# Five more dense U products ahead of the scatter, in homes taken from the scatter's share of memory

## The chip, the cores and the metric

The kernel runs on one core of a Trainium2 chip. The metric is the device time of one execution in microseconds (us). TensorE is called PE here, VectorE DVE, ScalarE ACT, GpSimd POOL, and SyncE, which issues most of the DMAs, SP.

## The reference, cut to what matters

One layer of a hybrid encoder over 512 tokens of width 1024: a mixer (RG-LRU and convolution), then PEER, a retrieval over 128 x 128 single-neuron experts, then a norm. The change touches PEER alone:

```python
q = (x @ w_q)                                    # 8 heads, 2 halves of 128
s = q . sub_keys                                 # 128 scores for each half
s1, i1 = top_k(s[:, :, 0], 16); s2, i2 = top_k(s[:, :, 1], 16)
top_s, pos = top_k(all s1 + s2, 16)              # 16 experts for each head and token
gate = softmax(top_s);  idx = 128 * i1 + i2
act = gelu(u[idx] . x)
out = sum over the 16 and the heads of gate * act * v[idx]
```

## The kernel before, in words

For 384 of the 512 tokens PEER is computed densely: for each of 128 columns of experts (128 experts each) a **U product** `gelu(u . x)` of 128 experts by 384 tokens, times a dense matrix of gates, times the V rows. The other 128 tokens gather their experts' rows one by one, later, beside the dense V loop. The trunk is in float32 precision: each operand is split into a high and a low part, and a product is three matmuls for each of eight slices, so 24 matmuls of 384 columns.

The order of the work in the stretch around the change:

1. **Routing.** Sixteen half-heads hp. For each: `query` (24 matmuls of 512 columns), the scores, then `rank` on DVE (top 16 of each of four token blocks). Behind some of them `choose` merges two halves into experts and gates, on DVE, ACT and POOL. Its first step on ACT is the cast `ii` (line 511), which reads the ranks' result. `US[hp]` says how many U products are written behind the scores of hp, ahead of the `choose` that follows. With one at the start (`EARLY`) these are products u0 to u22. For a U product in the routing ACT casts the high part (`w_hi`, line 108), POOL subtracts the low part (`w_lo`, line 110), PE multiplies (lines 464 to 466), ACT applies gelu (line 473).
2. **Scatter.** 3 token blocks of 8 steps, 16 tokens each. `turned(b)` makes the operand `trb` of a block by three PE transposes (line 624); the second and third block's are made behind the fifth step of the block before. Each step builds one-hot matrices on DVE (`hot` line 647, twice; `oa` line 651, six times; two buffers each, one for eight tokens), multiplies them on PE (`p_g`, line 657, 48 matmuls), copies the result out on ACT (`stg`) and writes it to memory (`scr_g`, line 661). Behind each step stands one U product, until 46 are made: u23 to u45 behind steps 1 to 23. Here DVE makes `w_lo`, not POOL.
3. **Tail.** u46 to u50 behind the scatter, with `w_lo` on POOL again, while the gates `g_s` come back from `scr_g` (line 726). They can be loaded only when the last step is written.
4. **Dense V loop.** 128 turns: `weigh` multiplies a U product by its gates (line 730) and splits it (`wt_hi`, `wt_lo`); PE multiplies by V (`po`, line 758); a later U product follows in each turn.

U products live in SBUF until they are weighed. u0 to u7 use spare gather buffers, the rest one of 44 `homes`: the first `HOMES_NOW` in pool `wk` (`w_e`), which is there during the routing, the next in `wk2` (`w_f`), opened when the routing's memory is given back, the last three in `wk3` (`w_g`), behind the scatter. Three more buffer counts matter: `w_hi` and `w_lo` have three buffers, raw weights five, and the PSUM tile `p_e` two. `p_e` is shared by the U products and the transposes of `turned`.

Waits and the order on each engine's queue are made by the framework when the kernel is built: it takes what is written first as more urgent, and lets a later instruction go ahead where, by its own estimate of durations, the earlier one isn't ready. On the chip each engine then runs its queue strictly in that order.

Of the kernel before, what the change touches and what calls it, by code (L numbers as in the profile page):

```python
# [60 lines left out]
def tile_kernel(ctx, tc, x, par, wi, bd, kd, mg, wo, wq, keys, u_rows, v_rows, u_t, v_t, fg, ffg, sel, out):  # L61
# [384 lines left out]
    AHEAD_W = 2  # L446
    EARLY = 1

    US = (0, 0, 0, 1, 1, 2, 1, 2, 1, 2, 1, 2, 1, 2, 1, 5)
    us = {}  # L450

    HOMES = AHEAD_U + 1 - 8
    HOMES_NOW = 15

    LAG = AHEAD_U - HOMES - 3
    HOMES_END = 3
    homes = [(wk, "w_e", HOMES_NOW)]

    def dense_u(i, eng):
        hi, lo = split(load(u_t[i].rearrange("p c e -> p (c e)")), eng)  # L460
        p = ps_e.tile([P, TD], F32, name="p_e")
        for c in range(NC):
            cs = slice(c * P, (c + 1) * P)
            nc.tensor.matmul(p, hi[:, cs], m_hi[:, c, :TD], start=(c == 0), stop=False)  # L464
            nc.tensor.matmul(p, hi[:, cs], m_lo[:, c, :TD], start=False, stop=False)  # L465
            nc.tensor.matmul(p, lo[:, cs], m_hi[:, c, :TD], start=False, stop=(c == NC - 1))  # L466
        if i < len(spare):
            w = spare[i]
        else:
            k = (i - len(spare)) % HOMES  # L470
            pool, name, n = homes[(k >= HOMES_NOW) + (k >= HOMES - HOMES_END)]
            w = pool.tile([P, NT, GT], F32, name=name, bufs=n)
        nc.scalar.activation(flat(w), p, AF.Gelu_apprx_tanh)  # L473
        us[i] = w
# [21 lines left out]
    def rank(rp, v, i, src):  # L496
        s2 = rp.tile([P, NK], F32, name="s2")
        best16(v, i, src, s2)
# [58 lines left out]
    with ExitStack() as rt:  # L557
# [25 lines left out]
        for hp in range(16):  # L583
# [9 lines left out]
            for b in range(NB):  # L593
                rank(rp, v16[:, hp // 2, b, hp % 2], i16[:, hp // 2, b, hp % 2], s[:, b])
            for _ in range(US[hp]):
                dense_u(len(us), nc.gpsimd)
# [7 lines left out]
    wk2 = ctx.enter_context(tc.tile_pool(name="wk2", bufs=1))  # L604
    homes.append((wk2, "w_f", HOMES - HOMES_NOW - HOMES_END))
    TURN = 4
# [267 lines left out]
```

## Time and profile before

| | us |
|---|---|
| median of 3 runs | 1566.47 (1563.59 to 1568.61) |
| the profiled execution: time | 1564.53 |
| its span, first to last instruction | 1562.8 |

PE is busy 94% of the span, DVE 79%, ACT 41%, POOL 42%. Times inside the profile are us from the start of the span. Routing with U products runs from about 267 to 487, the scatter to about 669, the V loop from 689 to the end.

### The profile page before, as it was taken

How to read it: one execution, taken by the hardware profiler on the slowest of the kernel's cores; microseconds unless marked ns; L12 is line 12 of the kernel's file. 1: busy time of each engine (PE TensorE's matmuls, PEld its weight loads, DVE VectorE, ACT ScalarE, POOL GpSimd, SP SyncE). 2: the span in 40 equal slices, each digit the busy share in tenths (PEclk: the TensorE clock that was granted, in tenths of full speed). 3: DMA queues.
4: the chain of work that ended last, by engine and by line, in shares of the span. 5: the costliest groups of instructions: out<-in, count | busy, mean ns of one | idle time of the engine just before them, and what ended most of it. 6: DMA issues, size and time to landing. Idle time of an engine off the chain costs nothing.

```text
span 1562.8 us, 21636 instructions
## 1 busy us (share of the span) xinstructions
PE 1475.6 (94%) x7939; PEld 1294.8 (83%) x7939; DVE 1230.5 (79%) x2255; ACT 636.4 (41%) x937; POOL 653.0 (42%) x382
## 2 busy tenths in 40 slices
PE   5987889999988999999899999999999999999997
PEld 4764657899977889898799999999999999888886
DVE  6995745599999999948777787777777877777776
ACT  5458443344434554442233333333333333333333
POOL 3644722476551000144455555445444444444440
PEclk9998879999989999999899999999999999999999
DMA  6220412323223666589999899998989988777783
GB/s 235 87 75 14 174 42 96 114 101 103 88 96 113 224 209 230 209 254 368 334 325 344 295 340 302 334 325 301 347 300 345 320 308 308 284 276 275 263 290 134
DMA packets 137787, 358.69 MB, mean 230 GB/s; under 512 B 10064, under 2 KB 59472, under 8 KB 134352
## 3 DMA queue, kind: packets, MB, share of 16 engines
q1 hardware_dynamic: 100240, 222.03, 41.8%
q0 software_dynamic: 36864, 134.23, 23.4%
q8 instruction: 62, 1.02, 0.3%
q10 hardware_dynamic: 576, 1.05, 0.2%
q14 instruction: 45, 0.37, 0.1%
HBM read 327.91 MB, written 29.36 MB: 229 GB/s over the span
## 4 chain that ended last, share of the span: by engine, by line
PE 77%; DVE 15%; DMA 3%; ACT 2%; issue 2%; POOL 1%; SPq 0%; DVEq 0%; ACTq 0%; POOLq 0%
PE po L758 32%; PE p_e L464 10%; PE p_e L466 10%; PE p_e L465 10%; PE p_g L657 3%; DVE oa L651 2%; DMA g_s<-scr_g 2%; PE pq L573 2%; PE pq L575 2%; PE pq L574 2%; DVE w_lo L110 1%; DVE hot L647 1%; DVE pc L228 1%; PE pz L417 1%; PE pz L331 1%
## 5 line engine op out<-in xcount | busy, mean ns | idle before, releaser
L108 ACT CAST w_hi<-raw_t 128x1024 fp32r<-128x1024 f32 x302 | 316.0, 1050 | 399.0 <-PE p_e L465 255.1
L464 PE MATMUL p_e<-m_hi,w_hi 128*128 128x384 f32 x1024 | 352.6, 344 | 6.5 <-ACT w_e L473 5.7
L466 PE MATMUL p_e<-m_hi,w_lo 128*128 128x384 f32 x1024 | 349.8, 342 | 6.5 <-DVE w_lo L110 6.4
L465 PE MATMUL p_e<-m_lo,w_hi 128*128 128x384 f32 x1024 | 348.6, 340 | 0.3 <-DVE m_lo L142 0.3
L110 POOL TENSOR_TENSOR w_lo<-raw_t,w_hi 128x1024 fp32r<-128x1024 f32 x74 | 199.0, 2703 | 344.3 <-ACT w_hi L108 331.2
L679 POOL DMA_INDIRECT g_t<-in_u_rows,eidx x128 | 210.7, 1646 | 215.4 <-DVE g_t L691 175.3
L110 DVE TENSOR_TENSOR w_lo<-raw_t,w_hi 128x1024 fp32r<-128x1024 f32 x228 | 275.3, 1219 | 12.0 <-ACT w_hi L108 11.9
L679 POOL DMA_INDIRECT g_t<-in_v_rows,eidx x128 | 189.3, 1479 | 224.8 <-DVE acc L701 213.4
L758 PE MATMUL po<-w_hi,wt_hi 128*128 128x512 f32 x768 | 240.6, 393 | 0.0
L758 PE MATMUL po<-w_hi,wt_lo 128*128 128x512 f32 x768 | 239.4, 391 | 0.0
L758 PE MATMUL po<-w_lo,wt_hi 128*128 128x512 f32 x768 | 238.8, 390 | 0.0
L464 PEld LDWEIGHTS p_e<-m_hi,w_hi 128*128 128x128 f32 x1024 | 196.3, 192 | 10.9 <-ACT w_e L473 6.4
L466 PEld LDWEIGHTS p_e<-m_hi,w_lo 128*128 128x128 f32 x1024 | 195.8, 191 | 7.9 <-DVE w_lo L110 7.9
L465 PEld LDWEIGHTS p_e<-m_lo,w_hi 128*128 128x128 f32 x1024 | 195.9, 191 | 3.5 <-DVE m_lo L142 0.5
L758 PEld LDWEIGHTS po<-w_lo,wt_hi 128*128 128x128 f32 x768 | 144.1, 188 | 33.3 <-DVE w_lo L110 0.3
L758 PEld LDWEIGHTS po<-w_hi,wt_lo 128*128 128x128 f32 x768 | 144.3, 188 | 30.4
L691 DVE SCALAR_TENSOR_TENSOR g_t<-g_t,Xg 128x1024 f32<-128x1024 f32 x128 | 151.8, 1222 | 17.2 <-DMA g_t<-in_u_rows,eidx 17.2
L758 PEld LDWEIGHTS po<-w_hi,wt_hi 128*128 128x128 f32 x768 | 143.1, 188 | 25.0 <-ACT w_hi L108 0.2
L701 DVE SCALAR_TENSOR_TENSOR acc<-g_t,dots,acc 128x1024 f32<-128x1024 f32 x127 | 162.4, 1278 | 1.0 <-DMA g_t<-in_v_rows,eidx 1.0
L732 ACT CAST wt_hi<-w_f 128x384 fp32r<-128x384 f32 x69 | 35.4, 513 | 183.0 <-PE po L758 183.0
L734 DVE TENSOR_TENSOR wt_lo<-w_f,wt_hi 128x384 fp32r<-128x384 f32 x69 | 38.5, 558 | 88.6 <-ACT wt_hi L732 88.4
L651 DVE TENSOR_TENSOR oa<-hot,trb 128x1024 bf16<-128x1024 bf16 x144 | 92.2, 697 | 0.6
(220 smaller groups left out, 1911.8 us busy)
## 6 DMA issues: line engine op xcount, KB each, us to landing
raw_t<-in_u_t SPq DMA_DIRECT2D x128, 512.0 KB, 5.8
raw_t<-in_v_t SPq DMA_DIRECT2D x128, 512.0 KB, 5.3
scr_g<-stg SPq DMA_DIRECT2D x24, 1024.0 KB, 4.8
g_s<-scr_g SPq DMA_DIRECT2D x16, 1536.0 KB, 12.9
raw_t<-in_wi SPq DMA_DIRECT2D x16, 512.0 KB, 3.9
raw_t<-in_wq SPq DMA_DIRECT2D x16, 512.0 KB, 3.8
raw_t<-in_wo SPq DMA_DIRECT2D x8, 512.0 KB, 3.7
raw_t<-in_kd SPq DMA_DIRECT2D x6, 512.0 KB, 3.6
```

The source lines that it names most:

```text
L108: nc.scalar.copy(hi, t)
L110: eng.tensor_sub(lo, t, f(hi))
L464: nc.tensor.matmul(p, hi[:, cs], m_hi[:, c, :TD], start=(c == 0), stop=False)
L465: nc.tensor.matmul(p, hi[:, cs], m_lo[:, c, :TD], start=False, stop=False)
L466: nc.tensor.matmul(p, lo[:, cs], m_hi[:, c, :TD], start=False, stop=(c == NC - 1))
L651: nc.vector.tensor_tensor(oa[:, q], hot[:, 1], over(2 + q, 1), op=ALU.mult)
L657: nc.tensor.matmul(p[:, t, :], hot[:, 0, g, :, o], oa[:, q, g, :, o], start=(q == 0), stop=(q == 2))
L679: nc.gpsimd.indirect_dma_start(out=t, out_offset=None, in_=rows, in_offset=bass.IndirectOffsetOnAxis(ap=eidx[:, k // K, k % K:k % K + 1], ...
L691: nc.vector.scalar_tensor_tensor(t, t, 1.0, Xg, op0=ALU.mult, op1=ALU.mult, accum_out=dots[:, k:k + 1])
L701: nc.vector.scalar_tensor_tensor(acc, t, dots[:, k:k + 1], acc, op0=ALU.mult, op1=ALU.add)
L734: return whi, wlo, nc.vector.tensor_sub(wlo, flat(w), f(whi))
L758: nc.tensor.matmul(po[b][hf], lhs[:, bs], rhs[:, hf * 512:(hf + 1) * 512], start=(i == 0 and n == 0), stop=(i == NK - 1 and n == 2))
```

## The change

Two numbers:

```diff
-    US = (0, 0, 0, 1, 1, 2, 1, 2, 1, 2, 1, 2, 1, 2, 1, 5)
+    US = (0, 0, 0, 1, 1, 2, 1, 2, 1, 2, 1, 2, 1, 2, 1, 10)
     us = {}
 
     HOMES = AHEAD_U + 1 - 8
-    HOMES_NOW = 15
+    HOMES_NOW = 20
```

u23 to u27 are now written behind the last scores (hp 15), ahead of the last `choose` and of the scatter, with `w_lo` on POOL. Their homes are in `wk` (20 in place of 15), and `wk2` has 21 in place of 26; 44 in all, as before. Inside the scatter the products u28 to u45 stand behind steps 1 to 18, and steps 19 to 24 have none. u46 to u50 still stand behind the scatter.

## Rows read from the trace of the kernel before

**Rows 1.** The page's first part: busy time, share of span, instructions.

```profile
PE 1475.6 (94%) x7939; PEld 1294.8 (83%) x7939; DVE 1230.5 (79%) x2255; ACT 636.4 (41%) x937; POOL 653.0 (42%) x382
```

**Rows 2.** Windows: length, each engine's busy time (instructions), granted clock, DMA.

```profile
440.00:490.00 50.00, 37.01 (x180) 35.01 (x179) 47.62 (x225) 20.30 (x32) 16.40 (x10) 0.83 0.25 84
...
500.00:650.00 150.00, 147.56 (x1490) 137.18 (x1490) 148.08 (x191) 76.56 (x141) 2.57 (x1) 1.00 0.61 218
```

**Rows 3.** Timeline of ACT at the end of the routing: start, duration [idle before, releaser].

```profile
474.05 0.41 ACT L511 CAST ii<-i 128x128 bf16<-128x128 uint32 x1 [8.60 <-DVE i L494]
...
487.68 0.30 ACT L623 COPY src<-gate_d 128x128 f32<-128x128 f32 x1 [3.31 <-DVE key_d L548]
...
488.83 0.48 ACT L473 ACTIVATE w_e<-p_e 128x384 f32<-128x384 f32 x1
```

**Rows 4.** Timeline of PE in the same stretch.

```profile
475.85 0.69 PE L464 MATMUL p_e<-m_hi,w_hi 128*128 128x384 f32 x1 [3.42 <-ACT w_e L473]
476.34 0.52 PE L465 MATMUL p_e<-m_lo,w_hi 128*128 128x384 f32 x1
476.66 0.52 PE L466 MATMUL p_e<-m_hi,w_lo 128*128 128x384 f32 x1
...
486.85 0.34 PE L466 MATMUL p_e<-m_hi,w_lo 128*128 128x384 f32 x1
488.03 0.33 PE L624 MATMUL p_e<-ident,src 128*128 128x128 f32 x1 [0.84 <-ACT src L623]
...
490.60 0.33 PE L624 MATMUL p_e<-ident,src 128*128 128x128 f32 x1 [0.55 <-ACT src L623]
490.69 0.42 PE L464 MATMUL p_e<-m_hi,w_hi 128*128 128x384 f32 x1
```

**Rows 5.** Timeline of ACT: an operand made for `turned(1)`, and its use.

```profile
491.14 0.29 ACT L623 COPY src<-gate_d 128x128 f32<-128x128 f32 x1
...
521.31 0.49 ACT L473 ACTIVATE w_f<-p_e 128x384 f32<-128x384 f32 x1
521.68 0.29 ACT L625 ACTIVATE tr<-p_e 128x128 f32<-128x128 f32 x1
```

**Rows 6.** Timeline of DVE in the scatter: first step, last two steps.

```profile
485.75 1.22 DVE L110 TENSOR_TENSOR w_lo<-raw_t,w_hi 128x1024 fp32r<-128x1024 f32 x1
...
491.35 2.36 DVE L647 TENSOR_TENSOR hot<-iot,trb 128x2048 bf16<-128x2048 bf16 x2 [0.25 <-ACT trb L625]
...
647.72 3.22 DVE L647 TENSOR_TENSOR hot<-iot,trb 128x2048 bf16<-128x2048 bf16 x1
...
654.04 4.04 DVE L651 TENSOR_TENSOR oa<-hot,trb 128x1024 bf16<-128x1024 bf16 x3
...
662.32 1.90 DVE L651 TENSOR_TENSOR oa<-hot,trb 128x1024 bf16<-128x1024 bf16 x3
```

**Rows 7.** Timeline of POOL at the end of the scatter.

```profile
647.29 2.57 POOL L110 TENSOR_TENSOR w_lo<-raw_t,w_hi 128x1024 fp32r<-128x1024 f32 x1 [158.03 <-ACT w_hi L108]
654.30 2.64 POOL L110 TENSOR_TENSOR w_lo<-raw_t,w_hi 128x1024 fp32r<-128x1024 f32 x1 [4.44 <-ACT w_hi L108]
```

**Rows 8.** Timeline of ACT: a tail product's cast, and two tail products' gelus.

```profile
646.16 1.05 ACT L108 CAST w_hi<-raw_t 128x1024 fp32r<-128x1024 f32 x1 [3.45 <-PE p_e L465]
...
677.36 0.48 ACT L473 ACTIVATE w_f<-p_e 128x384 f32<-128x384 f32 x1
...
681.52 0.48 ACT L473 ACTIVATE w_f<-p_e 128x384 f32<-128x384 f32 x1
```

**Rows 9.** From the last step to the V loop: timelines of PE, SP, DVE.

```profile
665.19 2.93 PE L657 MATMUL p_g<-oa,hot 128*128 128x128 bf16 x48
...
688.81 0.62 PE L758 MATMUL po<-w_hi,wt_hi 128*128 128x512 f32 x2
...
669.16 0.38 SPq L661 DMA_DIRECT2D scr_g<-stg  x1
...
684.19 1.50 DVE L730 TENSOR_TENSOR g_t<-g_t,g_s 128x384 f32<-128x384 f32 x3 [19.97 <-DMA g_s<-scr_g]
```

## Prediction

> **What bounds the kernel now.** I read the page's shares first, then a table of windows, then each engine's timeline around the end of the routing and the end of the scatter. PE is busy 94% of the span [rows 1], so a saving has to show up as less idle PE time, or as PE at a higher clock. From 440 to 490, the end of the routing, PE is busy 37.0 of 50.0 us at a granted clock of 0.83; from 500 to 650, the scatter, 147.6 of 150 at 1.00, and DVE 148.1 of 150 [rows 2]. So 13.0 us of PE idleness and some half-clock time lie at the end of the routing, and the scatter has neither PE nor DVE to spare. This is the argument for the change: it takes five products out of a full stretch and writes them into one with holes.
>
> The timelines say why the holes are there. ACT stands still for 8.6 us in front of `ii`, the first step of the last `choose`, which waits for the ranks on DVE [rows 3]. Finished products wait behind it for their gelu, both `p_e` buffers are full, and PE can't go on (3.4 us idle until a gelu, then matmuls 0.32 us apart [rows 4]). The holes are not for want of U products: u20 to u22 were at hand and could not be taken. From 475.85 to the last matmul of u22 at 486.85 PE has no hole left; u22's gelu follows at 488.83 [rows 3, 4]. The last `choose` ends on DVE, and ACT's `src` copy for `turned(0)` comes at 487.68 [rows 3]. So u22 and the routing end together: there is no empty PE time behind u22 but the waits between the transposes, 0.84 + 0.55 us in the two rows shown.
>
> **The change part by part.**
>
> *Five products ahead of the scatter.* The first of three transposes of `turned(0)` starts at 488.03, and u23 only behind the third, at 490.69, though its `w_lo` was done by about 487 [rows 4, 6] and PE had idled between the transposes. The other blocks show the same: the `src` copy of the next block is made at 491.14, and its first transpose's result is read at 521.68, straight behind the gelu of u26 at 521.31, the product written just ahead of it [rows 5]. I read this as: `p_e` buffers are given out in written order. With the change u23 to u27 are written ahead of `turned(0)`, so its transposes come behind u27. A product takes 4.16 us on PE (gelus at 677.36 and 681.52 [rows 8]), five take 20.8. They start when u22's last matmul has gone in, 486.85 + 0.17 = 487.0, and end at 507.8. The first transpose moves from 488.0 to 507.9: **+19.9 us**. The feed keeps up: one ACT cast (1.05) and gelu (0.48) [rows 8] and one `w_lo` of about 2.6 on POOL [rows 7] for each, under 4.16. The five DMA loads keep their place in SP's queue and only the products' names change. POOL has no other product in that stretch. From about 489 to 511 DVE, which makes the scatter's pace, has nothing to do: `hot` waits for `trb`.
>
> *The scatter on DVE.* It runs from 491.35 to 662.32 + 1.90 = 664.2 [rows 6]. Five `w_lo` of 1.22 leave it: **-6.1 us** (the three made ahead of the first step, as the one at 485.75, are so in both kernels). Steps 1 to 18 keep their load on both engines, so nothing of the 19.9 is caught up there. In steps 19 to 24 PE has 48 `p_g` (2.93 us [rows 9]) against DVE's 2 `hot` of 1.18 and 6 `oa` of 0.63, 6.2 us by these rows: PE is half empty there, and the tail's products are what can fill it.
>
> *The tail's products on POOL.* When POOL makes a `w_lo`, DVE's scatter stands still: `hot` takes 3.22 in place of 1.18 and three `oa` 4.04 in place of 1.90 just where POOL has u46 and u47 [rows 6, 7], 2.0 and 2.1 us. A cast runs as soon as PE is through with the product three back: u46's at 646.16, with u43's matmuls done [rows 8]. In the new kernel u43 to u45 are through by step 18, so all five tail casts, and with them five `w_lo` on POOL, fall into steps 16 to 24: three more collisions of 2.1, **+6.3 us**. Bounds: 0 (the tail stays where it was) to 6.3; the row with the lead of three is the nearest, so 6.3. A rule of the Trainium skill speaks against this part (SBUF — State Buffer, section Who interferes with whom): a VectorE instruction with two SBUF inputs and a GpSimd one that reads SBUF block each other, and the one that comes second waits out the whole of the other. By it, as an estimate, a collision could cost all of POOL's 2.6 us, and the term would be 7.8; the rows' 2.1 stand in the sum.
>
> *From the last step to the V loop.* Write of the last step at 669.16, gates weighed from 684.19 [rows 9]: 15.0 us, as before. Five tail products, 5 x 4.16 = 20.8 us, filled the time to the first `po` at 688.81 exactly. In the new kernel they are done earlier, and `po` waits for `weigh` alone: the first product multiplied (1.50 for three) and cast, about 2 us behind the gates in place of 4.6: **-2.5 us** (0 to -3.5). PE has then stood idle some 15 us. After 3.4 us of idleness PE took 11.2 us for two products (475.85 to 487.0 [rows 4]) in place of 8.3: **+2.8 us** (0 to 2.8).
>
> *Homes.* u23 to u27 get `w_e` homes; the distance of reuse stays 44 products, and a home is written only when the gelu comes, where nothing waited for memory before. 0 us; if a `w_f` home waited for the routing's memory, it would be back by 488, long before u28's gelu.
>
> *Sum.* 19.9 - 6.1 + 6.3 - 2.5 + 2.8 = +20.4 us on the profiled execution's own 1564.5, so 1584.9, and I say 1585. That execution lies 1.9 us below the median shown. By the terms' bounds: low 19.9 - 6.1 + 0 - 3.5 + 0 = +10.3 (1575), high 19.9 - 6.1 + 6.3 + 0 + 2.8 = +22.9 (1587). The check by PE's idle time agrees in sign: the work is the same, and what the change adds is empty PE time in steps 19 to 24 and ahead of the V loop (6 x (6.2 - 2.9) = 20 and about 17, less 20.8 of tail products), against about 3 us before.
>
> **The rivals.**
>
> *The transposes slip past.* If a transpose gets a `p_e` buffer between two products, DVE starts at 491.35 as before, but `p_g` is written behind u23 to u27 and waits for them. DVE has buffers for two groups, one step, about 6 us, and stops until 507.8 + 5: the delay is 20.8 - 6 = 14 to 15 us, the sum +6 (no new collision, -3.5) to +15. For it: an order by estimates is not the chip's. Against: rows 5. About 1577, chance 0.18.
>
> *`p_g` overtakes the products.* If the scatter's matmuls go ahead of u23 to u27, the scatter runs on time and the five products trail behind it into the half-empty steps 19 to 24 (6 x 3.3 = 20 us of room, just enough). The tail still fills the wait for the gates, and the change does nothing: -6.1 to +3, about 1564. Against it: what is written first goes first. Chance 0.10.
>
> *The holes are filled (faster).* The five products move up into the 13.0 us of idleness and the half-clock time of the routing. Place: ACT's queue, where casts and gelus would have to stand ahead of `ii`. Price: the transposes late by some 3 us, -6.1, no new collision, -2.5: -5 to -6, about 1559. It decides from the point where u27's gelu comes before about 493. Against it: `p_e` and `w_hi` buffers were full while ACT stood, and a later product adds no buffer. Chance 0.08.
>
> *PE at half clock through steps 19 to 24.* PE's gaps there are 1 to 3 us in each step, and after the 3.4 us gap the matmuls came 0.32 apart in place of 0.17 [rows 4]. At that rate a step with a tail product is 5.5 + 7.7 = 13.2 us of PE against some 8.3 of DVE, five such steps +25: about 1609. Chance 0.06. The Trainium skill (TensorE: Matmul & The Clock Gate, section HAM oscillation — how this bites in real kernels) says that bursts with waits between them can lower the clock again at each wait; this trace shows the fall behind the 3.4 us gap [rows 4], and none from 500 to 650, where the clock is 1.00 [rows 2].
>
> **How the numbers follow.** The forecast, delay by the written order of `p_e`, has chance 0.58, its own range 1574 to 1589. The range of 1567 to 1592 holds it, most of the first rival (together near 0.75) and the edge of the second and fourth. The runs of this kernel spread by 0.3%, so within 0.3% (1561.8 to 1571.2) counts as the same: 0.10 for the second rival and 0.02 from the low end of the first. Faster 0.08. Slower the rest, 0.80.
>
> **What would show it.** Right: 20 `w_e` gelus before the first `hot`, with the three transposes behind the fifth new one at about 508; DVE idle some 20 us before the scatter; five POOL `w_lo` inside the last nine steps with a DVE instruction of 3 to 4 us at each; the last `scr_g` write near 689; PE idle over 10 us ahead of the first `po` at about 706 to 709. Wrong: transposes still near 488, `p_g` between the new products, or new casts ahead of `ii` on ACT.

## The result, and the profile after

The changed kernel takes 1582.45 us (median of 4 runs, 1581.75 to 1583.03), the kernel before, run beside it, 1566.65 (1563.59 to 1568.61): ratio 1.0102, 95% interval 1.0085 to 1.012, so 1.0% slower. The profiled executions are 1582.02 and 1564.53, their spans 1580.0 and 1562.8: the traces have to account for +17.2 us.

The page's first part after, against [rows 1]:

```profile
PE 1481.4 (94%) x7939; PEld 1295.4 (82%) x7939; DVE 1235.2 (78%) x2250; ACT 638.0 (40%) x937; POOL 654.6 (41%) x387
```

PE runs the same 7939 matmuls in 5.8 us more busy time, some of it at half clock; the rest of the loss is emptier PE. The stretches of after in the windows' columns of [rows 2]:

```profile
440.00:490.00 50.00, 39.24 (x196) 37.89 (x195) 46.64 (x222) 19.78 (x29) 19.81 (x12) 0.83 0.22 74
490.00:515.00 25.00, 22.80 (x131) 21.83 (x131) 7.56 (x9) 9.06 (x19) 8.79 (x4) 1.00 0.45 148
630.00:650.00 20.00, 17.09 (x145) 16.32 (x144) 19.05 (x21) 7.11 (x12) 5.00 (x2) 0.83 0.54 202
```

And the last of these stretches in the kernel before:

```profile
630.00:650.00 20.00, 20.00 (x212) 19.53 (x211) 19.89 (x25) 10.48 (x18) 2.57 (x1) 1.00 0.56 220
```

The first row is the stretch whose holes were to be filled: PE is busy 39.2 of 50 us in place of 37.0, at the same clock. Five products were written for it, and the work gained there is half of one; even that lies behind u22, not in the holes, since from 440 to 487 PE is busy 36.2 us in both kernels. The second row is where they went: PE works on while DVE, which paces the scatter, is busy 7.56 of 25 us. The third was 20.00 us of PE at 1.00 before, and is 17.09 at 0.83 now.

The handover from routing to scatter on ACT, to be read against [rows 3, 5]:

```profile
314.15 0.67 ACT L511 CAST ii<-i 128x256 bf16<-128x256 uint32 x1 [0.57 <-DVE i L494]
...
474.07 0.41 ACT L511 CAST ii<-i 128x128 bf16<-128x128 uint32 x1 [8.58 <-DVE i L494]
...
487.76 0.30 ACT L623 COPY src<-gate_d 128x128 f32<-128x128 f32 x1 [3.35 <-DVE key_d L548]
...
488.91 0.48 ACT L473 ACTIVATE w_e<-p_e 128x384 f32<-128x384 f32 x1
...
509.17 0.48 ACT L473 ACTIVATE w_e<-p_e 128x384 f32<-128x384 f32 x1
509.55 0.27 ACT L625 ACTIVATE tr<-p_e 128x128 f32<-128x128 f32 x1
```

Up to 488.91 nothing has moved: the routing's first `ii` (314.11 before), the same wait of 8.6 us in front of `ii`, the same `src` copy, the same gelu of u22. Then come the gelus of u23 to u27, the last at 509.17, and only behind it the first transpose's result. PE after:

```profile
507.98 0.34 PE L466 MATMUL p_e<-m_hi,w_lo 128*128 128x384 f32 x1
508.15 0.27 PE L624 MATMUL p_e<-ident,src 128*128 128x128 f32 x1
...
642.70 0.27 PE L657 MATMUL p_g<-oa,hot 128*128 128x128 bf16 x1 [2.52 <-DVE oa L651]
643.30 2.51 PE L657 MATMUL p_g<-oa,hot 128*128 128x128 bf16 x22 [0.34 <-DVE oa L651]
...
646.03 0.52 PE L465 MATMUL p_e<-m_lo,w_hi 128*128 128x384 f32 x1
646.35 0.52 PE L466 MATMUL p_e<-m_hi,w_lo 128*128 128x384 f32 x1
...
651.48 2.70 PE L657 MATMUL p_g<-oa,hot 128*128 128x128 bf16 x44
...
669.59 2.30 PE L657 MATMUL p_g<-oa,hot 128*128 128x128 bf16 x20
...
707.95 1.22 PE L758 MATMUL po<-w_hi,wt_hi 128*128 128x512 f32 x2 [10.15 <-ACT wt_hi L732]
...
714.07 0.62 PE L758 MATMUL po<-w_lo,wt_hi 128*128 128x512 f32 x2
...
755.14 0.44 PE L466 MATMUL p_e<-m_hi,w_lo 128*128 128x384 f32 x1 [1.55 <-DVE w_lo L110]
...
776.44 0.69 PE L466 MATMUL p_e<-m_hi,w_lo 128*128 128x384 f32 x1 [3.43 <-DVE w_lo L110]
```

The first transpose starts 0.17 us behind the last matmul of u27, 20.1 us later than in [rows 4]. DVE after, against [rows 6, 9]:

```profile
511.62 2.36 DVE L647 TENSOR_TENSOR hot<-iot,trb 128x2048 bf16<-128x2048 bf16 x2 [0.20 <-ACT trb L625]
...
639.20 4.05 DVE L651 TENSOR_TENSOR oa<-hot,trb 128x1024 bf16<-128x1024 bf16 x3
...
653.06 3.07 DVE L647 TENSOR_TENSOR hot<-iot,trb 128x2048 bf16<-128x2048 bf16 x1 [3.68 <-PE p_g L657]
...
688.04 1.22 DVE L110 TENSOR_TENSOR w_lo<-raw_t,w_hi 128x1024 fp32r<-128x1024 f32 x1
689.18 1.89 DVE L651 TENSOR_TENSOR oa<-hot,trb 128x1024 bf16<-128x1024 bf16 x3
...
706.79 1.50 DVE L730 TENSOR_TENSOR g_t<-g_t,g_s 128x384 f32<-128x384 f32 x3 [6.79 <-DMA g_s<-scr_g]
```

POOL's five tail subtractions after, against [rows 7]:

```profile
632.57 2.46 POOL L110 TENSOR_TENSOR w_lo<-raw_t,w_hi 128x1024 fp32r<-128x1024 f32 x1 [133.31 <-DMA scr_g<-stg]
639.55 2.55 POOL L110 TENSOR_TENSOR w_lo<-raw_t,w_hi 128x1024 fp32r<-128x1024 f32 x1 [4.53 <-ACT w_hi L108]
652.67 2.38 POOL L110 TENSOR_TENSOR w_lo<-raw_t,w_hi 128x1024 fp32r<-128x1024 f32 x1 [10.57 <-ACT w_hi L108]
665.13 2.43 POOL L110 TENSOR_TENSOR w_lo<-raw_t,w_hi 128x1024 fp32r<-128x1024 f32 x1 [10.08 <-ACT w_hi L108]
677.80 2.52 POOL L110 TENSOR_TENSOR w_lo<-raw_t,w_hi 128x1024 fp32r<-128x1024 f32 x1 [10.23 <-ACT w_hi L108]
```

SP's queue, the write of the last step:

```profile
693.20 0.32 SPq L661 DMA_DIRECT2D scr_g<-stg  x1
```

Put together, event by event:

| event | before | after | late by | this step adds |
|---|---|---|---|---|
| first transpose on PE | 488.03 | 508.15 | 20.1 | +20.1 |
| first `hot` on DVE | 491.35 | 511.62 | 20.3 | +0.2 |
| last `oa` ends | 664.22 | 691.07 | 26.9 | +6.6 |
| last `scr_g` write issued | 669.16 | 693.20 | 24.0 | -2.8 |
| gates multiplied | 684.19 | 706.79 | 22.6 | -1.4 |
| first `po` | 688.81 | 707.95 | 19.1 | -3.5 |
| end of the span | 1562.8 | 1580.0 | 17.2 | -1.9 |

The last row holds two things: seven pairs of `po` at half pace (707.95 to 714.07, 6.1 us in place of 7 x 0.46 = 3.2), +2.9, and so 4.8 us that the V loop gives back.

### The profile page after: what moved, and what is told of

Its sections match the earlier page's. It is cut to its first block, busy times and chain, and to the rows that moved or that the text cites. A ratio compares the mean times of both kernels' runs of the same rounds, so it can differ in the third digit from the quotient of the medians.

```text
span 1580.0 us, 21629 instructions
## 1 busy us (share of the span) xinstructions
PE 1481.4 (94%) x7939; PEld 1295.4 (82%) x7939; DVE 1235.2 (78%) x2250; ACT 638.0 (40%) x937; POOL 654.6 (41%) x387
## 4 chain that ended last, share of the span: by engine, by line
PE 75%; DVE 15%; DMA 3%; ACT 2%; issue 2%; POOL 1%; SPq 0%; DVEq 0%; POOLq 0%; ACTq 0%
PE po L758 31%; PE p_e L466 9%; PE p_e L464 9%; PE p_e L465 9%; DVE oa L651 3%; PE p_g L657 2%; DMA g_s<-scr_g 2%; DVE hot L647 2%; PE pq L573 2%; PE pq L574 2%; PE pq L575 2%; DVE pc L228 1%; PE pz L417 1%; PE pz L331 1%; PE pz L329 1%
## 5 line engine op out<-in xcount | busy, mean ns | idle before, releaser
L110 POOL TENSOR_TENSOR w_lo<-raw_t,w_hi 128x1024 fp32r<-128x1024 f32 x79 | 211.4, 2688 | 337.6 <-ACT w_hi L108 191.1
L679 POOL DMA_INDIRECT g_t<-in_u_rows,eidx x128 | 199.3, 1557 | 243.7 <-DVE g_t L691 176.1
L110 DVE TENSOR_TENSOR w_lo<-raw_t,w_hi 128x1024 fp32r<-128x1024 f32 x223 | 269.4, 1220 | 36.0 <-ACT w_hi L108 35.9
L758 PE MATMUL po<-w_hi,wt_hi 128*128 128x512 f32 x768 | 242.0, 395 | 10.2 <-ACT wt_hi L732 10.2
L691 DVE SCALAR_TENSOR_TENSOR g_t<-g_t,Xg 128x1024 f32<-128x1024 f32 x128 | 152.4, 1222 | 22.6 <-DMA g_t<-in_u_rows,eidx 22.4
L651 DVE TENSOR_TENSOR oa<-hot,trb 128x1024 bf16<-128x1024 bf16 x144 | 97.1, 730 | 0.9
L732 ACT CAST wt_hi<-w_e 128x384 fp32r<-128x384 f32 x60 | 30.8, 513 | 160.2 <-PE po L758 160.2
L657 PE MATMUL p_g<-oa,hot 128*128 128x128 bf16 x1152 | 84.7, 223 | 8.3 <-DVE oa L651 8.0
```

Source lines behind the costliest of these rows:

```text
L110: eng.tensor_sub(lo, t, f(hi))
L651: nc.vector.tensor_tensor(oa[:, q], hot[:, 1], over(2 + q, 1), op=ALU.mult)
L657: nc.tensor.matmul(p[:, t, :], hot[:, 0, g, :, o], oa[:, q, g, :, o], start=(q == 0), stop=(q == 2))
L679: nc.gpsimd.indirect_dma_start(out=t, out_offset=None, in_=rows, in_offset=bass.IndirectOffsetOnAxis(ap=eidx[:, k // K, k % K:k % K + 1], ...
L691: nc.vector.scalar_tensor_tensor(t, t, 1.0, Xg, op0=ALU.mult, op1=ALU.mult, accum_out=dots[:, k:k + 1])
L758: nc.tensor.matmul(po[b][hf], lhs[:, bs], rhs[:, hf * 512:(hf + 1) * 512], start=(i == 0 and n == 0), stop=(i == NK - 1 and n == 2))
```

## The experiments

All times are medians, beside runs of the kernel before on the same chip (1565.8 to 1566.9). The edits of the first four stand against the changed kernel.

**Is it the shared buffer?** The prediction said that the transposes wait for u27 because `p_e` buffers are given out in written order. Here they get a PSUM buffer of their own (and `p_g` five in place of six).

```diff
-            p = ps_e.tile([P, P], F32, name="p_e")
+            p = ps_r.tile([P, P], F32, name="p_r")
...
```

> The changed kernel, with one PSUM buffer of their own for the three transposes of turned (ps_g has five buffers in place of six). If the transposes came late because the p_e buffers are given out in written order, they now start near 488, first hot near 491.5, p_g waits for the products up to u27 and the time falls by 4 to 6 us to about 1577. If the written order alone makes PE take u23 to u27 first (they are ready and more urgent), the buffer changes nothing: transposes near 508, time 1582 within 3 us.

1580.84, ratio 1.0099 (1.0082 to 1.0116). PE of this kernel:

```profile
509.63 0.27 PE L624 MATMUL p_r<-ident,src 128*128 128x128 f32 x1
```

Its `src` copy is at 489.22, its buffer is free, and the transpose still stands behind u27 on PE, 20 us later. The buffer isn't what holds it; PE's queue has the five products first.

**The transposes first.** The five products are written behind `turned(0)`, ahead of the scatter.

```diff
-    US = (0, 0, 0, 1, 1, 2, 1, 2, 1, 2, 1, 2, 1, 2, 1, 10)
+    US = (0, 0, 0, 1, 1, 2, 1, 2, 1, 2, 1, 2, 1, 2, 1, 5)
...
         trb = turned(0)
+        for _ in range(5):
+            dense_u(len(us), nc.gpsimd)
```

> The changed kernel, with u23 to u27 written behind turned(0) and ahead of step 1 in place of behind the last scores. Order theory: transposes near 488 and first hot near 491.5 as in the kernel before; DVE makes about one step and stops, since p_g stands behind u27 on PE (until about 512); scatter late by some 14 us in place of 20, time about 1576 (1573 to 1580). If the late transposes were the whole cost: 1563 to 1566. If the cost lay in the tail's products and not in the start: 1582.

1581.37, ratio 1.0099 (1.0082 to 1.0116): the medians show nothing won (15.6 us over the kernel beside it, where the changed kernel had 15.8). ACT, DVE and PE of this kernel, the first row, the routing's first `ii`, against 314.15 in the changed one:

```profile
317.02 0.68 ACT L511 CAST ii<-i 128x256 bf16<-128x256 uint32 x1 [0.56 <-DVE i L494]
```

```profile
497.02 2.35 DVE L647 TENSOR_TENSOR hot<-iot,trb 128x2048 bf16<-128x2048 bf16 x2
499.29 5.90 DVE L651 TENSOR_TENSOR oa<-hot,trb 128x1024 bf16<-128x1024 bf16 x6
...
518.44 2.35 DVE L647 TENSOR_TENSOR hot<-iot,trb 128x2048 bf16<-128x2048 bf16 x2
```

```profile
493.60 0.33 PE L624 MATMUL p_e<-ident,src 128*128 128x128 f32 x1 [0.55 <-ACT src L623]
...
516.15 2.92 PE L657 MATMUL p_g<-oa,hot 128*128 128x128 bf16 x48
```

Now the written order puts the transposes first, at 491 to 494, and DVE does step 1 ahead of time. But its next `hot` needs the buffers that `p_g` frees, and `p_g` stands behind the five products, at 516.15. Step 2 begins at 518.44; in the changed kernel it begins at 517.51. PE's products end 8.0 us later than there. This execution had lost 2.9 of that by its first `ii`, 170 us ahead of the stretch; the rest is the transposes with their waits, which now lie ahead of the products, and some ten matmuls at half clock behind them (from 494.91). It eats most of the step's lead: counted from the first `ii`, step 2 begins 1.9 us sooner than in the changed kernel and the last `oa` ends 3.0 sooner (at 690.95), too little for the medians to tell. So what costs is, for the most part, not the place of three transposes but five products' PE time ahead of the scatter's first PE result, wherever exactly it stands.

**The tail's subtractions on DVE,** with nothing else changed:

```diff
-        dense_u(len(us), nc.gpsimd)
+        dense_u(len(us), nc.vector)
```

> The changed kernel, with w_lo of the tail's products u46 to u50 on DVE in place of POOL. Collision theory (each POOL w_lo stops DVE's scatter for 2.1 us): five of 2.1 go, five w_lo of 1.15 to 1.22 come, so -4 us: 1578 (1576 to 1580). If the collisions are hidden behind PE: 1582 or, with DVE's extra work, up to 1585.

1577.83, ratio 1.0079 (1.0062 to 1.0096): 12.0 us over the kernel beside it, where the changed kernel had 15.8. The two intervals overlap, so the gain of 3.8 is likely, not certain. Groups of DVE by line inside the scatter (busy us, mean ns | idle before), first the changed kernel, then this one:

```profile
L651 DVE TENSOR_TENSOR oa<-hot,trb 128x1024 bf16<-128x1024 bf16 x144 | 97.1, 730 | 0.9
L647 DVE TENSOR_TENSOR hot<-iot,trb 128x2048 bf16<-128x2048 bf16 x48 | 61.9, 1297 | 4.1 <-PE p_g L657 3.9 <-ACT trb L625 0.2
L110 DVE TENSOR_TENSOR w_lo<-raw_t,w_hi 128x1024 fp32r<-128x1024 f32 x16 | 19.5, 1219 | 1.4 <-ACT w_hi L108 1.4
```

```profile
L651 DVE TENSOR_TENSOR oa<-hot,trb 128x1024 bf16<-128x1024 bf16 x144 | 90.4, 687 | 0.6
L647 DVE TENSOR_TENSOR hot<-iot,trb 128x2048 bf16<-128x2048 bf16 x48 | 57.9, 1220 | 0.2 <-ACT trb L625 0.2
L110 DVE TENSOR_TENSOR w_lo<-raw_t,w_hi 128x1024 fp32r<-128x1024 f32 x22 | 26.9, 1221 | 1.6 <-ACT w_hi L108 1.6
```

DVE does six subtractions more (+7.4 us) and is through with the scatter 9.3 us sooner (170.1 us from the first `hot` to the last `oa`, in place of 179.5): `oa` and `hot` lose 10.7 us of stretching, and the wait of 3.9 us for `p_g` is gone; that makes 7.2 of the 9.3, and the rest I didn't place. About half of the 9.3 reaches the end (the spans are 1575.0 and 1580.0); part of the other half shows in front of the V loop, where PE waits longer for the gates (14.28 us in place of 10.15).

**Products back into the last steps.** The changed kernel with no product behind steps 1 to 6, so that u28 to u45 stand behind steps 7 to 24:

```diff
-            if len(us) < AHEAD_U - HOMES_END - 2:
+            if len(us) < AHEAD_U - HOMES_END - 2 and b * 8 + t0 // GT >= 6:
```

> The changed kernel, with no product behind the scatter's steps 1 to 6 in place of steps 19 to 24; the tail's five products should then stay behind the scatter as in the kernel before. Order theory: first hot still near 511.5 (+20), five w_lo less on DVE (-6), two collisions as before, no idle PE ahead of the V loop and no slow start: +14, 1579 to 1580. If the tail's early products and the idle PE ahead of the V loop cost nothing: 1582.

1578.53, ratio 1.0087 (1.007 to 1.0103). The time is as expected, the mechanism only in part: PE's wait ahead of `po` shrinks from 10.15 to 1.61 us and the slow start is gone, but POOL's tail subtractions didn't stay behind the scatter (they stand at 648.86, 661.09, 670.98, 681.77 and 692.71): four of the five meet DVE there, where two were expected.

**How the cost grows with the products moved.** Seven and four products behind hp 15, against 5 before and 10 after (`HOMES_NOW` 17 and 14):

```diff
-    US = (0, 0, 0, 1, 1, 2, 1, 2, 1, 2, 1, 2, 1, 2, 1, 10)
+    US = (0, 0, 0, 1, 1, 2, 1, 2, 1, 2, 1, 2, 1, 2, 1, 7)
...
```

> The changed kernel with two more products in place of five (last entry of US 7, HOMES_NOW 17). Order theory: each product behind u22 puts the transposes off by 4.16 us and takes 1.2 off DVE, so the cost is in proportion: first hot near 499.7 (+8.3), time +6 to +7 over before, about 1572 to 1573. If the holes at the end of the routing take the first two products for nothing: 1564 to 1566.

1569.39 (1564.15 to 1571.37, ten runs), ratio 1.0019 (1.0007 to 1.0031). The start of the scatter moved as expected, first `hot` at 499.38, 8.0 us late, and the gates at 693.04 are 8.9 late. Yet the median is only 2.5 above that of the kernel beside it, where 6 were expected: the loss at the front of the scatter isn't carried whole to the end.

> The kernel before with one product less ahead of the scatter (last entry of US 4, HOMES_NOW 14; all 24 steps of the scatter then have a product). Order theory: the scatter can't start before the last choose ends on DVE (487.6), so nothing is won at the start and about 4 us of PE time ahead of the transposes stay empty; DVE gets 1.2 more: +1 to +4 over before, 1567 to 1570. If the cost were in proportion below five as well: 1562 to 1563.

1568.76, ratio 1.0019 (1.0008 to 1.003), as expected: with fewer than five, nothing is won either, since the scatter can't start before the last `choose`. In this trace the last `choose` ends even later than before, its `key_d` at 491.18 in place of 487.20 (1.8 of that lost by the first `ii`), which wasn't expected.

**The holes themselves.** The holes in PE's queue stand behind ACT's wait for `ii`. Here DVE makes `ii` for the last two `choose`, first in the kernel before, then in the changed one:

```diff
-        nc.scalar.copy(ii, i[:, hh].rearrange("p h b t k -> p t k (h b)"))
+        (nc.scalar.copy if n > 1 else nc.vector.tensor_copy)(ii, i[:, hh].rearrange("p h b t k -> p t k (h b)"))
```

> The kernel before with the cast ii of the last two chooses on DVE in place of ACT; the order on PE stays. Theory that ACT's wait for ranks makes PE's holes: the hole at 472 to 476 shrinks or goes and u22 ends earlier, some 3 to 6 us, but the scatter still waits for the last choose on DVE (487.6 plus about 0.3), so the time stays within 2 us of before. If more than that is won, PE's lateness at the start of the scatter counted too.

> The changed kernel with the cast ii of the last two chooses on DVE in place of ACT; the order on PE stays. Theory that ACT's wait for ranks makes PE's holes and u23 to u27 come only behind u22: u22 ends 3 to 8 us earlier and with it u27 and the transposes: first hot near 503 to 508, time 3 to 8 us under the changed kernel, 1574 to 1579. If PE's holes come from something else (buffers, the gelus behind other waits of ACT): 1582 within 2.

1568.89, ratio 1.0013 (1.0 to 1.0026), and 1589.85, ratio 1.0159 (1.0134 to 1.0184): the second is 7.2 us worse than the changed kernel, each against the kernel beside it, where a gain was expected. ACT and PE of the second:

```profile
458.07 0.26 ACT L551 ACTIVATE gate_d<-gate_d 128x64 f32<-128x64 f32 x1 [14.87 <-POOL gate_d L550]
...
483.28 0.26 ACT L551 ACTIVATE gate_d<-gate_d 128x64 f32<-128x64 f32 x1 [7.70 <-POOL gate_d L550]
```

```profile
460.67 2.08 PE L588 MATMUL p_s<-ky,q 128*128 128x128 f32 x8 [9.55 <-ACT q L577]
...
486.24 0.69 PE L464 MATMUL p_e<-m_hi,w_hi 128*128 128x384 f32 x1 [4.98 <-ACT w_e L473]
```

The wait didn't go, it moved to ACT's next step of the same `choose`, the Exp of the gates, with the casts and gelus still behind it. PE's gaps there are 9.55 and 4.98 us; in the changed kernel they are 7.36 (at 456.56) and 3.40 (at 475.86). The first of the two runs has the same gaps (9.56 and 5.07), so its hole didn't shrink either; its time came out as expected, its mechanism did not. So the holes belong to the order of ACT's queue around `choose`, as far as these rows go, not to one instruction in it, and my theory of them fell. Why the same edit costs 7.2 us in one kernel and 2.0 in the other stays open.

**Homes alone.** The kernel before with one of the two numbers:

```diff
-    HOMES_NOW = 15
+    HOMES_NOW = 20
```

> The kernel before with HOMES_NOW 20 alone (US as before): the homes move, no product does. Order theory: 0, within 0.3% of before (1562 to 1571). If homes taken from wk2 cost something by themselves (a wait for the routing's memory, or for a home's reuse in the V loop): slower by 3 us or more.

1566.28, ratio 1.0 (0.9991 to 1.0009): the move in memory costs nothing.

**What the collisions cost without the change.** The kernel before with the tail on DVE (the diff of tail_on_vector), and the same with seven and with six products behind hp 15 (`HOMES_NOW` 17 and 16):

> The kernel before with w_lo of the tail's five products on DVE in place of POOL. Collision theory: the two collisions inside the scatter go (each 2.1 us, against 1.15 for a w_lo of DVE's own), and with them the gap in which PE's clock fell: -2 to -4, 1563 to 1565. If the V loop's start is what sets the end (five products must be through PE by then), 0 to -1.

> Two products more ahead of the scatter (US 7, HOMES_NOW 17) and w_lo of the tail on DVE. The run with seven alone was 2.5 over before with three collisions in the scatter; without them -2 to -4: 1565 to 1568, near before. If the collisions are hidden there: 1569.

> One product more ahead of the scatter (US 6, HOMES_NOW 16) and w_lo of the tail on DVE. Order theory: transposes late by about 4 us, -1.2 on DVE, collisions gone: about the same as five with the tail on DVE, 1563 to 1567.

1560.20, ratio 0.996 (0.9947 to 0.9973); 1558.07, ratio 0.9954 (0.994 to 0.9968); 1557.71, ratio 0.9949 (0.9936 to 0.9962). All three beat both kernels, by more than was expected; they aren't told apart from each other. The prices that I had used, 2.1 us for each collision less 1.22 for the subtraction on DVE, make 1.8 for the two collisions of [rows 6]; 6.3 were measured (4.2 to 8.3 by the interval). The traces show less: the spans are 1561.5 and 1562.8, and as this execution stood 1.4 us later at its first `ii` (315.53), 2.7 were won from there on. A stretch at the scatter's end shows what the prices leave out, in the windows' columns, first of the kernel before, then with its tail on DVE:

```profile
650.00:670.00 20.00, 17.01 (x152) 16.28 (x151) 14.08 (x16) 7.10 (x12) 5.02 (x2) 0.91 0.48 161
```

```profile
650.00:670.00 20.00, 20.00 (x212) 19.68 (x210) 16.50 (x22) 10.38 (x18) 0.00 (x0) 1.00 0.58 212
```

PE of the kernel before in that stretch:

```profile
657.54 0.22 PE L657 MATMUL p_g<-oa,hot 128*128 128x128 bf16 x1 [2.52 <-DVE oa L651]
658.14 1.48 PE L657 MATMUL p_g<-oa,hot 128*128 128x128 bf16 x22 [0.38 <-DVE oa L651]
...
659.85 0.52 PE L465 MATMUL p_e<-m_lo,w_hi 128*128 128x384 f32 x1
660.17 0.52 PE L466 MATMUL p_e<-m_hi,w_lo 128*128 128x384 f32 x1
...
755.00 0.69 PE L464 MATMUL p_e<-m_hi,w_hi 128*128 128x384 f32 x1 [2.27 <-ACT w_e L473]
759.05 0.69 PE L466 MATMUL p_e<-m_hi,w_lo 128*128 128x384 f32 x1 [3.04 <-DVE w_lo L110]
```

The collision that stretches `oa` leaves PE without work for 2.52 us, and the product behind it runs about half of its matmuls 0.32 us apart in place of 0.17, at 1.2 in place of 2.4 GHz. It is the same picture, to the hundredth of the gap, as at 642.70 of the changed kernel. With the tail on DVE that gap isn't there, the clock stays at 1.00, and PE does by busy time and clock about 20.0 - 17.0 x 0.91 = 4.5 us more work in these 20 us (an estimate from the two rows). Part of that is lost elsewhere: in this run 15 matmuls behind the first transposes come at half clock (from 492.31), and in the kernel before none.

## Why the prediction was right, and where its steps were off

1585.0 was forecast, 1582.45 measured, inside the forecast's own range and on the side that was given 0.80. Step by step:

- **The products push the scatter back:** +19.9 forecast, +20.1 measured. The reason given for it, that `p_e` buffers are given out in written order, failed: with a buffer of its own the first transpose comes no sooner (own_psum), and with `turned(0)` written first it does, on the shared buffer (turned_first). What is shown is that PE's queue has the products in the order in which they are written. [Rows 5], on which I rested, are the same order seen from the buffer.
- **The first rival's price fell with that.** I gave it -6 us for the step that DVE would do ahead. turned_first makes that case: counted from the first `ii`, its trace wins 1.9 us at step 2 and 3.0 at the last `oa`, and its median nothing that can be told. Left out of the price were the transposes and their waits ahead of the products, and the clock's fall behind them.
- **The collisions:** five in the scatter, as forecast, 1.9 to 2.2 us each above the undisturbed row; the five sum to 10.2 against 4.1 for the two of [rows 6], so +6.0 for +6.3. The Trainium skill (SBUF — State Buffer, section Who interferes with whom) says that the instruction that comes second waits out the whole of the other; the trace agrees. In all five DVE's instruction begins 0.2 to 0.4 us behind POOL's (`hot` at 632.95 and 653.06, single `oa` at 639.81, 665.37 and 677.98), and what it loses, 2.0 us on the mean, is to 0.2 us what is then left of POOL's 2.4 to 2.6. The prediction's 7.8 by that rule took POOL's instruction whole, where its rest is what counts.
- **The scatter's length is the term that was mis-sized:** +6.6 in place of -6.1 + 6.3 = +0.2. The larger part is the collision's second price, which I had left out though before has the same gap: PE starves for 2.52 us, falls to half clock for 22 `p_g` and about half of a product, the next step's `p_g` comes late at 651.48, and DVE waits 3.68 us for its buffers. Then DVE's subtractions fell by four (20 to 16), not five, because one for a V weight moved in (at 688.04): -4.8. Together -4.8 + 6.0 + 3.7 = +4.9. Of the last 1.7 some 1.2 (an estimate) lie in DVE's order: 20 steps in place of 15 take `hot` and `oa` by turns, and such a step without a subtraction lasts 6.14 us (657.98 to 664.12), where one with both `hot` first lasts 5.88 (627.62 to 634.64 before, less 1.14 for its subtraction); with a subtraction among them the difference is 0.12.
- **The clock.** The fourth rival's mechanism is there twice, from 643 to 649 (22 `p_g` in 2.51 us, then matmuls 0.32 apart) and from 669.6 to 673 (20 `p_g` in 2.30 us, behind a gap of 1.97), not through steps 19 to 24, and so at a small part of its price. The Trainium skill (TensorE: Matmul & The Clock Gate, section HAM oscillation — how this bites in real kernels) says that a burst followed by a wait can lower the clock each time; the trace agrees for the gap of 2.52 us with the 0.34 behind it and for that of 1.97, and shows most steps of the scatter without a fall, one with a gap of 1.94 (at 656.92) among them.
- **From the last step to the V loop:** the write stands 2.8 us nearer to the last `oa` than before, where a product, in part at half clock, had held `p_g` up; 15.0 us from write to gates became 13.6; neither was in the sum. `po` came 1.2 behind the gates in place of 4.6: -3.5, the end of its bounds, for -2.5. The slow start was +2.9 for +2.8, behind 10.15 us of idleness in place of some 15.
- **What the sum had no term for:** the early V loop gave back 4.8 us. In the first 70 us or so of that loop PE waits four times in either kernel: 8.7 us in the kernel before (2.32, 1.04, 2.27 and 3.04, the last two at 755.00 and 759.05 above) and 6.3 in the changed one (0.56, 1.55, 0.73 and 3.43, the last at 776.44), and some 29 matmuls come at half clock there before and 18 after, about 1.5 us less. Together that is 3.9 of the 4.8. No run shows that it comes from the change: homes_alone, which moves no product, waits 12.9 us there. us_seven's median too is less late than its scatter; its profiled execution, 1564.15, is the fastest of its ten, so I don't size it there.

The errors on the path have both signs: +6.4 in the scatter, -2.8, -1.4, -1.0 and -4.8 behind it. That the size came out well is in part luck: they cancel.

**Open.** Why the V loop's waits differ (up to 800, 8.7 us in the kernel before, 12.9 in homes_alone, 7.9 in tail_on_vector, 6.3 in the changed kernel, 5.7 in us_seven): the queues are planned anew with each edit, single executions differ as well, and no run isolates one wait. That the half-clock product explains the 6.3 us of before_tail_vector is argued from the windows and the like gaps of three kernels (us_seven has it too, 2.52 us at 651.53); its own trace shows 2.7, and no run takes the clock's fall away and leaves the collision. The traces stand up to 4 us apart by the routing's first `ii` already (313.5 in us_seven, 317.5 in before_ii_dve), ahead of the stretch that was changed; why is open, and two traces are best compared from such a common event.

## What to carry to other kernels

Before moving work into another stage's holes, ask what makes them: here ACT's in-order queue, standing in front of `choose`, and more products written there couldn't get in but queued up ahead of the next stage's first PE result, at their full 4.16 us each. Price a collision of two engines by what starves behind it too, the third engine's gap, its clock and the buffers that it frees late. An operation that takes 1.22 us on the full engine can be cheaper there than 2.5 us on an idle one that blocks it: this, not the change, gave the best versions (before_tail_vector, six_tail_vector and seven_tail_vector, 0.4 to 0.5% faster than before and not told apart).

## What the runs showed of the hardware

Behind a gap of 2.52 us with a second of 0.34 or 0.38, in the kernel before and in the changed one, PE fell to 1.2 GHz, for some 3.5 us there and 6 here; I had looked at the gap of 3.4 us in [rows 4] alone. The length of one gap doesn't settle it: in the changed kernel PE fell behind a gap of 1.97 us (at 668.17) and not behind one of 1.94 (at 656.92). And POOL's subtraction of 128 x 1024 delays DVE's two-input operations by 1.9 to 2.2 us wherever it meets them in these two kernels' scatters, by as much as is left of it when they begin, against 1.22 us for the same subtraction on DVE.
